# Hardware loops on ScalarE and VectorE, counts taken down by PE, 8-row casts and shared set-up buffers in a LoRA projection that moves 67 MB

## Chip, cores, metric

The kernel runs on one core of one Trainium2 chip. The metric is device time in microseconds (us), the median over executions. The profile's span (first to last instruction of the program) is about 1.3 us shorter than the time.

## The reference

```python
# x: 16 x 2048 x 256 f32 (32768 rows), W: 256 x 256, A: 256 x 16, B: 16 x 256, E: 16, scale = 1.0
y = x @ W + scale * (((x @ lora_A) * lora_E) @ lora_B)      # f32, 33.5 MB in and 33.5 MB out
```

The kernel folds the small factors into one matrix, weff = W + A·diag(E)·scale·B, once. Then it computes y = x·weff.

## The kernel before

The rows are cut into 4 chunks of 64 rows in each of 128 partitions. A chunk (8.39 MB) has a "home" in SBUF. x is loaded there, the result is written over it, and it is stored from there. There are three homes, so chunk 3 must wait for stores of chunk 0. All loads and stores are issued by SyncE in a fixed order.

```python
ORDER = [("A",), ("L", 0, 0, 8), ("L", 0, 8, 24), ("L", 0, 24, 40), ("L", 0, 40, 64),
         ("L", 1, 0, 32), ("L", 1, 32, 64), ("L", 2, 0, 16), ("L", 2, 16, 64),
         ("S", 0, 0, 40), ("S", 0, 40, 64), ("L", 3, 0, 32), ("L", 3, 32, 64),
         ("S", 1, 0, 64), ("S", 2, 0, 64), ("S", 3, 0, 64)]     # kind, chunk, rows from, to
HELD = (2, 16)                       # GpSimd stops at row 16 of chunk 2 ...
HOLDERS = (("S", 0, 0, 40),)         # ... until this store has landed
CG = 4                               # rows of one group; 64 groups in all
```

Each group goes through five steps: GpSimd casts it to bf16, PE turns it (4 matmuls), VectorE copies it out of PSUM, PE multiplies it (8 matmuls), and ScalarE copies the result into the home.

```python
# GpSimd, 64 times (waits for loads and for the hold: cut)
gpsimd.wait_ge(s_turned, g - NS + 1)
gpsimd.tensor_copy(out=stage[g % NS][:], in_=home(c)[:, b:b + CG, :]).then_inc(s_stage[g % UNROLL], 1)
# ScalarE, written out 64 times
scalar.wait_ge(s_y, g + 1)
scalar.copy(out=home(c)[:, b:b + CG, :], in_=psum_y[g % NY][:]).then_inc(s_free[(g + NY) % UNROLL], 1)
if g in ends:
    scalar.drain().then_inc(s_done, 1)          # releases a store
# PE, a hardware loop of 16 laps
with tensor.Fori(0, N_GROUPS // UNROLL):
    for i in range(UNROLL):
        turn(i + 1, i)
        multiply(i)
```

Of the kernel before, what the change touches and what calls it, by code (L numbers as in the profile page):

```python
# [7 lines left out]
P = 128  # L8
FP32 = mybir.dt.float32
BF16 = mybir.dt.bfloat16  # L10
# [3 lines left out]
ROWS = 64  # L14
N_CHUNKS = 4
N_HOMES = 3

ORDER = [
    ("A",),
    ("L", 0, 0, 8),  # L20
    ("L", 0, 8, 24),
    ("L", 0, 24, 40),
    ("L", 0, 40, 64),
    ("L", 1, 0, 32),
    ("L", 1, 32, 64),
    ("L", 2, 0, 16),
# [13 lines left out]
WARM_UP = 2  # L40

CG = 4
GPC = ROWS // CG
N_GROUPS = N_CHUNKS * GPC

NS, NX, NT, NY = 2, 2, 2, 2

UNROLL = 4
# [3 lines left out]
def kernel(  # L52
# [20 lines left out]
    y_chunks = out_flat.rearrange("(c p b) m -> c p b m", p=P, b=ROWS)  # L73

    sbuf, psum, sem = nc.alloc_sbuf_tensor, nc.alloc_psum_tensor, tc.alloc_semaphore
    homes = [sbuf(f"home{h}", [P, ROWS, K], FP32) for h in range(N_HOMES)]
    stage = [sbuf(f"stage{i}", [P, CG, K], BF16) for i in range(NS)]
    xt = [sbuf(f"xt{i}", [P, CG, P * KT], BF16) for i in range(NX)]
    ident = sbuf("ident", [P, P], FP32)

    w_sb = sbuf("w_sb", [P, KT, M], FP32)
    a_sb = sbuf("a_sb", [P, KT, R], FP32)
    b_sb = sbuf("b_sb", [R, M], FP32)
    e_sb = sbuf("e_sb", [R, 1], FP32)
    ate = sbuf("ate", [R, KT, P], FP32)
    weff = sbuf("weff", [P, KT, M], BF16)
    psum_xt = [psum(f"psum_xt{i}", [P, CG, P], FP32) for i in range(NT)]
    psum_y = [psum(f"psum_y{i}", [P, CG, M], FP32) for i in range(NY)]
# [8 lines left out]
    stored = {op: sem(f"stored_{op[1]}_{op[2]}") for op in ORDER if op in waited}  # L97
    stored_rest = nc.alloc_semaphore("stored_rest")
    n_rest = sum(op[0] == "S" and op not in waited for op in ORDER)
    ends = sorted((c * ROWS + e) // CG - 1 for kind, c, s, e in (op for op in ORDER if op[0] == "S"))  # L100
    s_ident = sem("ident_made")
    s_pe_set_up = sem("pe_set_up")
    s_ate = sem("ate_made")
    s_stage = [sem(f"staged{i}") for i in range(UNROLL)]
    s_turned = sem("turned")
    s_xt = [sem(f"xt_made{i}") for i in range(UNROLL)]
    s_y = sem("multiplied")
    s_free = [sem(f"y_free{i}") for i in range(UNROLL)]
    s_done = sem("rows_done")

    def home(c):
        return homes[c % N_HOMES]

    sync, gpsimd, scalar, vector, tensor = nc.sync, nc.gpsimd, nc.scalar, nc.vector, nc.tensor

# [19 lines left out]
    def sync_program():  # L135
        for n, op in enumerate(ORDER):
            if op[0] == "A":
                a = lora_A.rearrange("(q t) r -> q t r", t=KT)
                ins = sync.dma_start(out=a_sb[:], in_=a).then_inc(set_up_loaded["a"], 16)
                opening.append(ins.ins.name)  # L140
                continue
            kind, c, s, e = op
            at_home = home(c)[:, s:e, :]
            if kind == "L":
                for st in stored:
                    if st[1] == c - N_HOMES and st[2] < e and s < st[3]:
                        sync.wait_ge(stored[st], 16)
                ins = sync.dma_start(out=at_home, in_=x_chunks[c, :, s:e, :]).then_inc(loaded[op], 16)
                if n == 1:
                    opening.append(ins.ins.name)  # L150
            else:
                sync.wait_ge(s_done, ends.index((c * ROWS + e) // CG - 1) + 1)
                sync.dma_start(out=y_chunks[c, :, s:e, :], in_=at_home).then_inc(stored.get(op, stored_rest), 16)

    def gpsimd_program():
        gpsimd.memset(ident[:], 0.0).then_inc(s_ident, 1)  # L156
        gpsimd.wait_ge(s_ident, 1)
        gpsimd.affine_select(  # L158
            out=ident[:],
            in_=ident[:],  # L160
            compare_op=ALU.not_equal,
            fill=1.0,
            base=0,
            pattern=[[-1, P]],
            channel_multiplier=1,
        ).then_inc(s_ident, 1)
        for g in range(N_GROUPS):
            c, b = g // GPC, g % GPC * CG
            for op, landed in loaded.items():
                if op[1:3] == (c, b):  # L170
                    gpsimd.wait_ge(landed, 16)
            if (c, b) == HELD:
                for op in HOLDERS:
                    gpsimd.wait_ge(stored[op], 16)
            if g >= NS:
                gpsimd.wait_ge(s_turned, g - NS + 1)  # L176
            gpsimd.tensor_copy(out=stage[g % NS][:], in_=home(c)[:, b:b + CG, :]).then_inc(s_stage[g % UNROLL], 1)  # L177

        gpsimd.wait_ge(s_turned, N_GROUPS - NS + 1)
        gpsimd.drain().then_inc(s_stage[N_GROUPS % UNROLL], 1)  # L180

    def scalar_program():
        for name, to, of in (
            ("w", w_sb, W.rearrange("(q t) m -> q t m", t=KT)),
            ("b", b_sb, lora_B),
            ("e", e_sb, lora_E[:, None]),
        ):
            ins = scalar.dma_start(out=to[:], in_=of).then_inc(set_up_loaded[name], 16)
            opening.append(ins.ins.name)
        for g in range(N_GROUPS):  # L190
            c, b = g // GPC, g % GPC * CG
            scalar.wait_ge(s_y, g + 1)
            scalar.copy(out=home(c)[:, b:b + CG, :], in_=psum_y[g % NY][:]).then_inc(s_free[(g + NY) % UNROLL], 1)  # L193
            if g in ends:
                scalar.drain().then_inc(s_done, 1)  # L195

    def vector_program():
        vector.wait_ge(set_up_loaded["e"], 16)
        vector.wait_ge(s_pe_set_up, 1)
        vector.tensor_scalar(  # L200
            out=ate[:],
            in0=psum_y[0][:R, :KT, :P],
            scalar1=e_sb[:],
            scalar2=float(scale),
            op0=ALU.mult,
            op1=ALU.mult,
        ).then_inc(s_ate, 1)
        for g in range(N_GROUPS):
            vector.wait_ge(s_turned, g + 1)
            vector.tensor_copy(out=xt[g % NX][:], in_=psum_xt[g % NT][:].bitcast(BF16)).then_inc(s_xt[g % UNROLL], 1)  # L210
            if g == 0:
                vector.wait_ge(set_up_loaded["w"], 16)
                vector.wait_ge(s_pe_set_up, 2)
                vector.tensor_add(out=weff[:], in0=w_sb[:], in1=psum_y[1][:, :KT, :]).then_inc(s_free[0], 1)  # L214
                vector.drain().then_inc(s_free[1], 1)

    def tensor_program():
        def turn(i, result=None):
            words = stage[i % NS][:].bitcast(FP32)
            staged = s_stage[i % UNROLL]  # L220
            for b in range(CG):
                if b == 0:
                    tensor.wait_ge(staged, 1)
                if b == CG - 1 and result is not None:
                    tensor.wait_ge(s_free[result % UNROLL], 1)
                ins = tensor.transpose(psum_xt[i % NT][:, b, :], words[:, b, :], ident[:])  # L226
                if b == 0:
                    ins.then_inc(staged, -1)
            ins.then_inc(s_turned, 1)

        def multiply(i):
            turned, free = s_xt[i % UNROLL], s_free[i % UNROLL]
            for b in range(CG):
                for t in range(KT):
                    if b == t == 0:
                        tensor.wait_ge(turned, 1)
                    ins = tensor.matmul(  # L237
                        psum_y[i % NY][:, b, :],
                        xt[i % NX][:, b, t::KT],
                        weff[:, t, :],  # L240
                        start=(t == 0),
                        stop=(t == KT - 1),
                    )
                    if b == 0:
                        ins.then_inc((turned, free)[t], -1)
            ins.then_inc(s_y, 1)

        tensor.wait_ge(s_ident, 2)
        for i in range(WARM_UP):
            tensor.matmul(psum_y[1][:, :2, :], ident[:], ident[:, None, :].to_broadcast([P, 4, P]), start=True, stop=True)  # L250
        tensor.wait_ge(set_up_loaded["a"], 16)
        for t in range(KT):
            ins = tensor.transpose(psum_y[0][:R, t, :P], a_sb[:, t, :], ident[:])  # L253
        ins.then_inc(s_pe_set_up, 1)
        turn(0)
        tensor.wait_ge(set_up_loaded["b"], 16)
        tensor.wait_ge(s_ate, 1)
        for t in range(KT):
            ins = tensor.matmul(psum_y[1][:, t, :], ate[:, t, :], b_sb[:], start=True, stop=True)  # L259
        ins.then_inc(s_pe_set_up, 1)  # L260
        assert N_GROUPS % UNROLL == 0 and all(UNROLL % n == 0 for n in (NS, NX, NT, NY))
        with tensor.Fori(0, N_GROUPS // UNROLL):
            for i in range(UNROLL):
                turn(i + 1, i)
                multiply(i)

    def wait_for_stores(nc):
        nc.sync.wait_ge(stored_rest, 16 * n_rest).then_inc(stored_rest, -16 * n_rest)
# [44 lines left out]
```

## Time and profile before

| what | value | where |
|---|---|---|
| time, first 3 runs | 161.38 us (161.38 to 161.85) | timing |
| moved | 67.43 MB in all; the data queue takes 97.2% of 16 transfer engines' time | page, parts 2 and 3 |
| rate, 3 to 157 us | 433 GB/s | windows |
| PE busy | 59% of the span | page, part 1 |
| ScalarE per group | 1012 ns, then 0.30 us idle | groups, timeline |

From the page of the kernel before: the span, then, for 40 equal slices, the busy tenths of PE, ScalarE (ACT) and the mean of the 16 transfer engines, and the line of the data queue (packets, MB, share of 16 engines' span).

```profile
span 161.5 us, 2024 instructions
...
PE   2988999969999990000899999999910000000000
...
ACT  3003677747777772000157777777730000000000
...
DMA  7999999999999997998999999799799799699690
...
q1 hardware_dynamic: 2304, 67.13, 97.2%
```

The transfers are busy throughout. Compute stops twice: in the hold (about 62 to 76 us), and for good in the last quarter.

The timeline of SyncE's queue (start, length, what) shows when stores and the held loads were issued. A later window of the same view put the third of the last three stores at 118.69 us.

```profile
27.66 9.87 SPq L153 DMA_DIRECT2D out_dram<-home  x2
75.94 7.69 SPq L148 DMA_DIRECT2D home<-in_x_dram  x2
83.68 35.34 SPq L153 DMA_DIRECT2D out_dram<-home  x3
```

The last store is issued when about 19 us of earlier stores are still to be moved, by the prediction's estimate.

### The profile page before, as it was taken

The numbers are of one execution on the slowest core, as the hardware profiler recorded it, in microseconds if no ns is written. First come the engines' busy times: TensorE is split into PE (matmuls) and PEld (weight loads), VectorE is DVE, ScalarE is ACT, GpSimd is POOL, SyncE is SP. The second block draws the span as 40 slices with busy tenths as digits, with TensorE's granted clock in tenths as the row PEclk, the third lists the DMA queues.
The fourth block names the chain that finished last, engine by engine and source line by source line (L and its number), as shares of the span: only waits on it lengthen the run. The fifth ranks groups of instructions, "written<-read, shape, count | busy, mean of one in ns | idle before, by whom it ended". The sixth has DMA issues, their size and how long they took to land.

```text
span 161.5 us, 2024 instructions
## 1 busy us (share of the span) xinstructions
PE 95.4 (59%) x782; PEld 83.4 (52%) x782; DVE 45.4 (28%) x66; ACT 66.1 (41%) x65; POOL 66.9 (41%) x70
## 2 busy tenths in 40 slices
PE   2988999969999990000899999999910000000000
PEld 1347999959999990000789989999900000000000
DVE  0141555535555550000155555555400000000000
ACT  3003677747777772000157777777730000000000
POOL 1516768577778840001578777788200000000000
PEclk9975999999999999555599999999996555555555
DMA  7999999999999997998999999799799799699690
GB/s 253 405 438 452 402 452 446 446 406 446 394 548 414 402 390 337 477 467 371 420 459 440 406 446 536 319 519 471 308 503 487 308 503 503 292 503 503 292 519 16
DMA packets 2515, 67.43 MB, mean 418 GB/s; under 512 B 448, under 2 KB 464, under 8 KB 592
## 3 DMA queue, kind: packets, MB, share of 16 engines
q1 hardware_dynamic: 2304, 67.13, 97.2%
q10 hardware_dynamic: 208, 0.28, 0.6%
q14 instruction: 3, 0.02, 0.0%
HBM read 33.85 MB, written 33.55 MB: 417 GB/s over the span
## 4 chain that ended last, share of the span: by engine, by line
DMA 36%; PE 34%; POOL 1%; ACT 1%; issue 0%; SPq 0%; ACTq 0%; POOLq 0%
DMA out_dram<-home 30%; PE psum_y L237 22%; PE psum_xt L226 12%; DMA home<-in_x_dram 6%; POOL stage L177 1%; ACT home L193 1%; ACTq L195 0%; SPq L308 0%; POOLq L176 0%; SPq L272 0%
## 5 line engine op out<-in xcount | busy, mean ns | idle before, releaser
L193 ACT COPY home<-psum_y 128x1024 f32<-128x1024 f32 x64 | 64.8, 1012 | 50.5 <-PE psum_y L237 50.5
L177 POOL CAST stage<-home 128x1024 bf16<-128x1024 f32 x64 | 66.2, 1042 | 44.8 <-DMA out_dram<-home 17.5
L237 PE MATMUL psum_y<-weff,xt 128*128 128x256 bf16 x512 | 69.6, 281 | 0.0
L210 DVE COPY xt<-psum_xt 128x1024 bf16<-128x1024 bf16 x64 | 44.3, 692 | 63.4 <-PE psum_xt L226 63.4
L237 PEld LDWEIGHTS psum_y<-weff,xt 128*128 128x128 bf16 x512 | 51.8, 101 | 6.5
L226 PE MATMUL psum_xt<-ident,stage 128*128 128x128 f32 x260 | 41.4, 283 | 19.3 <-POOL stage L177 19.0
L226 PEld LDWEIGHTS psum_xt<-ident,stage 128*128 128x128 f32 x260 | 31.5, 146 | 22.1 <-issue 20.7
L250 PE MATMUL psum_y<-ident 128*128 128x512 f32 x4 | 3.7, 1078 | 2.9 <-POOL ident L158 2.9
L250 PEld LDWEIGHTS psum_y<-ident 128*128 128x128 f32 x4 | 1.2, 324 | 3.9 <-POOL ident L158 2.9
L200 DVE TENSOR_SCALAR ate<-psum_y,e_sb 16x256 f32<-16x256 f32 x1 | 0.5, 472 | 6.9 <-PE psum_y L253 6.9
L193 ACT ACT_TABLE_LOAD x1 | 1.3, 1283 | 2.1 <-SPq L272 2.1
L259 PE MATMUL psum_y<-b_sb,ate 16*128 16x256 f32 x4 | 1.1, 400 | 0.0
L156 POOL MEMSET ident<- 128x128 f32 x1 | 0.2, 205 | 1.7 <-SPq L272 1.7
L253 PEld LDWEIGHTS psum_y<-ident,a_sb 128*16 128x16 f32 x2 | 0.2, 114 | 1.2 <-issue 1.2
L214 DVE TENSOR_TENSOR weff<-w_sb,psum_y 128x512 bf16<-128x512 f32 x1 | 0.7, 687 | 0.4 <-PE psum_y L259 0.4
L259 PEld LDWEIGHTS psum_y<-b_sb,ate 16*128 16x128 f32 x4 | 0.7, 184 | 0.2 <-issue 0.2
L158 POOL TENSOR_SCALAR_AFFINE_SELECT ident<-ident 128x128 f32<-128x128 f32 x1 | 0.3, 293 | 0.2 <-POOL ident L156 0.2
L253 PE MATMUL psum_y<-ident,a_sb 128*16 128x128 f32 x2 | 0.4, 273 | 0.0
L294 POOL MEMSET const-float32-0.0<- 128x1 f32 x1 | 0.1, 99 | 0.2 <-issue 0.2
L294 POOL MEMSET const-bfloat16-1.0<- 128x1 bf16 x1 | 0.1, 103 | 0.0
L294 POOL MEMSET const-uint8-127<- 128x1 uint8 x1 | 0.1, 103 | 0.0
L294 POOL MEMSET const-float32-1.0<- 128x1 f32 x1 | 0.1, 99 | 0.0
## 6 DMA issues: line engine op xcount, KB each, us to landing
home<-in_x_dram SPq DMA_DIRECT2D x4, 4096.0 KB, 25.1
home<-in_x_dram SPq DMA_DIRECT2D x3, 2048.0 KB, 13.8
home<-in_x_dram SPq DMA_DIRECT2D x1, 6144.0 KB, 58.9
out_dram<-home SPq DMA_DIRECT2D x1, 5120.0 KB, 48.3
home<-in_x_dram SPq DMA_DIRECT2D x1, 3072.0 KB, 20.7
out_dram<-home SPq DMA_DIRECT2D x1, 3072.0 KB, 46.0
home<-in_x_dram SPq DMA_DIRECT2D x1, 1024.0 KB, 5.4
w_sb<-in_W_dram ACTq DMA_DIRECT2D x1, 256.0 KB, 3.0
```

Of the source, the lines that this page charges most:

```text
L158: gpsimd.affine_select(out=ident[:], in_=ident[:], compare_op=ALU.not_equal, fill=1.0, base=0, pattern=[[-1, P]], channel_multiplier=1,).t ...
L177: gpsimd.tensor_copy(out=stage[g % NS][:], in_=home(c)[:, b:b + CG, :]).then_inc(s_stage[g % UNROLL], 1)
L193: scalar.copy(out=home(c)[:, b:b + CG, :], in_=psum_y[g % NY][:]).then_inc(s_free[(g + NY) % UNROLL], 1)
L200: vector.tensor_scalar(out=ate[:], in0=psum_y[0][:R, :KT, :P], scalar1=e_sb[:], scalar2=float(scale), op0=ALU.mult, op1=ALU.mult,).then_in ...
L210: vector.tensor_copy(out=xt[g % NX][:], in_=psum_xt[g % NT][:].bitcast(BF16)).then_inc(s_xt[g % UNROLL], 1)
L214: vector.tensor_add(out=weff[:], in0=w_sb[:], in1=psum_y[1][:, :KT, :]).then_inc(s_free[0], 1)
L226: ins = tensor.transpose(psum_xt[i % NT][:, b, :], words[:, b, :], ident[:])
L237: ins = tensor.matmul(psum_y[i % NY][:, b, :], xt[i % NX][:, b, t::KT], weff[:, t, :], start=(t == 0), stop=(t == KT - 1),)
L250: tensor.matmul(psum_y[1][:, :2, :], ident[:], ident[:, None, :].to_broadcast([P, 4, P]), start=True, stop=True)
L253: ins = tensor.transpose(psum_y[0][:R, t, :P], a_sb[:, t, :], ident[:])
L259: ins = tensor.matmul(psum_y[1][:, t, :], ate[:, t, :], b_sb[:], start=True, stop=True)
L294: nc = _bacc.Bacc("TRN2", target_bir_lowering=False, num_devices=1)
```

## The change

The intent is a shorter program. ScalarE and VectorE run hardware loops whose waits are constants, because PE takes each count down again. PE also counts finished rows, which removes ScalarE's drains. GpSimd casts 8 rows at a time, and set-up tensors use a stage buffer that is still free. The core of the diff (set-up and renaming cut):

```diff
-    homes = [sbuf(f"home{h}", [P, ROWS, K], FP32) for h in range(N_HOMES)]
-    stage = [sbuf(f"stage{i}", [P, CG, K], BF16) for i in range(NS)]
+    ring = sbuf("ring", [P, RING, K], FP32)
+    stage = [sbuf(f"stage{i}", [P, CAST, K], BF16) for i in range(NS)]          # CAST = 8
+    spare = stage[1][:].bitcast(FP32)...                                        # w_sb, b_sb, ate live here
...
-                sync.wait_ge(s_done, ends.index((c * ROWS + e) // CG - 1) + 1)
+                sync.wait_ge(s_done, (c * ROWS + e) // CG + NY)
...
-            scalar.wait_ge(s_y, g + 1)
-            scalar.copy(out=home(c)[:, b:b + CG, :], in_=psum_y[g % NY][:]).then_inc(...)
-            if g in ends:
-                scalar.drain().then_inc(s_done, 1)
+        for n in (RING, N_CHUNKS * ROWS - RING):
+            with scalar.Fori(0, n // (UNROLL * CG)) as lap:
+                for i in range(UNROLL):
+                    scalar.wait_ge(s_y[i], 1)
+                    to = ring[:, bass.ds(lap * (UNROLL * CG) + i * CG, CG), :]
+                    scalar.copy(out=to, in_=psum_y[i % NY][:]).then_inc(s_free[(i + NY) % UNROLL], 1)
...
+        with vector.Fori(0, N_GROUPS // UNROLL):
...
+            updates = {                                  # of multiply(i), by matmul
+                (0, 1): (s_xt[i % UNROLL], -1), (1, 0): (s_free[i % UNROLL], -1),
+                (1, 1): (s_turned[i % UNROLL], -1), (2, 0): (s_y[(i - NY) % UNROLL], -1),
+                (2, 1): (s_done, 1), (3, 1): (s_y[i % UNROLL], 1)}
```

More of the change, by code (lines that the diff above doesn't have):

```diff
@@ L42 @@
 CG = 4
-GPC = ROWS // CG
-N_GROUPS = N_CHUNKS * GPC
+CAST = 2 * CG
+RING = N_HOMES * ROWS
+N_GROUPS = N_CHUNKS * ROWS // CG
 NS, NX, NT, NY = 2, 2, 2, 2
@@ L75 @@
     sbuf, psum, sem = nc.alloc_sbuf_tensor, nc.alloc_psum_tensor, tc.alloc_semaphore
-    homes = [sbuf(f"home{h}", [P, ROWS, K], FP32) for h in range(N_HOMES)]
-    stage = [sbuf(f"stage{i}", [P, CG, K], BF16) for i in range(NS)]
+    ring = sbuf("ring", [P, RING, K], FP32)
+    stage = [sbuf(f"stage{i}", [P, CAST, K], BF16) for i in range(NS)]
     xt = [sbuf(f"xt{i}", [P, CG, P * KT], BF16) for i in range(NX)]
     ident = sbuf("ident", [P, P], FP32)
-    w_sb = sbuf("w_sb", [P, KT, M], FP32)
     a_sb = sbuf("a_sb", [P, KT, R], FP32)
-    b_sb = sbuf("b_sb", [R, M], FP32)
     e_sb = sbuf("e_sb", [R, 1], FP32)
-    ate = sbuf("ate", [R, KT, P], FP32)
+    spare = stage[1][:].bitcast(FP32).rearrange("q (n s) k -> q n (s k)", s=2)
+    w_sb, b_sb, ate = spare[:, :KT, :], spare[:R, 2, :], spare[:R, 3, :].rearrange("r (t q) -> r t q", t=KT)
     weff = sbuf("weff", [P, KT, M], BF16)
@@ L99 @@
     n_rest = sum(op[0] == "S" and op not in waited for op in ORDER)
-    ends = sorted((c * ROWS + e) // CG - 1 for kind, c, s, e in (op for op in ORDER if op[0] == "S"))
     s_ident = sem("ident_made")
@@ L103, with rows @@
     s_ate = sem("ate_made")
-    s_stage = [sem(f"staged{i}") for i in range(UNROLL)]
-    s_turned = sem("turned")
+    s_weff = sem("weff_made")
+    s_stage = [sem(f"staged{i}") for i in range(NS)]
+    s_room = sem("stage_read")
+    s_turned = [sem(f"turned{i}") for i in range(UNROLL)]
     s_xt = [sem(f"xt_made{i}") for i in range(UNROLL)]
-    s_y = sem("multiplied")
+    s_y = [sem(f"multiplied{i}") for i in range(UNROLL)]
     s_free = [sem(f"y_free{i}") for i in range(UNROLL)]
     s_done = sem("rows_done")
-    def home(c):
-        return homes[c % N_HOMES]
+    def rows(c, s, e):
+        at = c % N_HOMES * ROWS
+        return ring[:, at + s:at + e, :]
     sync, gpsimd, scalar, vector, tensor = nc.sync, nc.gpsimd, nc.scalar, nc.vector, nc.tensor
@@ L142, in sync_program @@
             kind, c, s, e = op
-            at_home = home(c)[:, s:e, :]
+            at_home = rows(c, s, e)
             if kind == "L":
@@ L166, in gpsimd_program @@
         ).then_inc(s_ident, 1)
-        for g in range(N_GROUPS):
-            c, b = g // GPC, g % GPC * CG
+        n_casts = N_CHUNKS * ROWS // CAST
+        for n in range(n_casts):
+            c, b = n * CAST // ROWS, n * CAST % ROWS
             for op, landed in loaded.items():
@@ L174, in gpsimd_program @@
                     gpsimd.wait_ge(stored[op], 16)
-            if g >= NS:
-                gpsimd.wait_ge(s_turned, g - NS + 1)
-            gpsimd.tensor_copy(out=stage[g % NS][:], in_=home(c)[:, b:b + CG, :]).then_inc(s_stage[g % UNROLL], 1)
-        gpsimd.wait_ge(s_turned, N_GROUPS - NS + 1)
-        gpsimd.drain().then_inc(s_stage[N_GROUPS % UNROLL], 1)
+            if n == 1:
+                gpsimd.wait_ge(s_weff, 1)
+            if n >= NS:
+                gpsimd.wait_ge(s_room, n - NS + 1)
+            gpsimd.tensor_copy(out=stage[n % NS][:], in_=rows(c, b, b + CAST)).then_inc(s_stage[n % NS], 1)
+        gpsimd.wait_ge(s_room, n_casts - NS + 1)
+        gpsimd.drain().then_inc(s_stage[n_casts % NS], 1)
     def scalar_program():
@@ L185, in scalar_program @@
             ("b", b_sb, lora_B),
-            ("e", e_sb, lora_E[:, None]),
+            ("e", e_sb[:], lora_E[:, None]),
         ):
-            ins = scalar.dma_start(out=to[:], in_=of).then_inc(set_up_loaded[name], 16)
+            ins = scalar.dma_start(out=to, in_=of).then_inc(set_up_loaded[name], 16)
             opening.append(ins.ins.name)
-        for g in range(N_GROUPS):
-            c, b = g // GPC, g % GPC * CG
-            scalar.wait_ge(s_y, g + 1)
-            scalar.copy(out=home(c)[:, b:b + CG, :], in_=psum_y[g % NY][:]).then_inc(s_free[(g + NY) % UNROLL], 1)
-            if g in ends:
-                scalar.drain().then_inc(s_done, 1)
+        for n in (RING, N_CHUNKS * ROWS - RING):
[4 more added lines that the diff above has]
+                    scalar.copy(out=to, in_=psum_y[i % NY][:]).then_inc(s_free[(i + NY) % UNROLL], 1)
     def vector_program():
@@ L200, in vector_program @@
         vector.tensor_scalar(
-            out=ate[:],
+            out=ate,
             in0=psum_y[0][:R, :KT, :P],
@@ L207, in vector_program @@
         ).then_inc(s_ate, 1)
-        for g in range(N_GROUPS):
-            vector.wait_ge(s_turned, g + 1)
-            vector.tensor_copy(out=xt[g % NX][:], in_=psum_xt[g % NT][:].bitcast(BF16)).then_inc(s_xt[g % UNROLL], 1)
-            if g == 0:
-                vector.wait_ge(set_up_loaded["w"], 16)
-                vector.wait_ge(s_pe_set_up, 2)
-                vector.tensor_add(out=weff[:], in0=w_sb[:], in1=psum_y[1][:, :KT, :]).then_inc(s_free[0], 1)
-                vector.drain().then_inc(s_free[1], 1)
+        vector.wait_ge(s_turned[0], 1)
@@ new lines, in vector_program @@
+        vector.tensor_copy(out=xt[0][:], in_=psum_xt[0][:].bitcast(BF16)).then_inc(s_xt[0], 1)
+        vector.wait_ge(set_up_loaded["w"], 16)
+        vector.wait_ge(s_pe_set_up, 2)
+        vector.tensor_add(out=weff[:], in0=w_sb, in1=psum_y[1][:, :KT, :]).then_inc(s_free[0], 1)
+        vector.drain().then_inc(s_weff, 1)
+        with vector.Fori(0, N_GROUPS // UNROLL):
+            for i in range(UNROLL):
+                g = i + 1
+                vector.wait_ge(s_turned[g % UNROLL], 1)
+                vector.tensor_copy(out=xt[g % NX][:], in_=psum_xt[g % NT][:].bitcast(BF16)).then_inc(s_xt[g % UNROLL], 1)
@@ L217, in tensor_program @@
     def tensor_program():
         def turn(i, result=None):
-            words = stage[i % NS][:].bitcast(FP32)
-            staged = s_stage[i % UNROLL]
+            n, at = divmod(i, CAST // CG)
+            words = stage[n % NS][:].bitcast(FP32)
             for b in range(CG):
-                if b == 0:
-                    tensor.wait_ge(staged, 1)
+                if b == 0 and at == 0:
+                    tensor.wait_ge(s_stage[n % NS], 1)
                 if b == CG - 1 and result is not None:
@@ L225, in turn @@
                     tensor.wait_ge(s_free[result % UNROLL], 1)
-                ins = tensor.transpose(psum_xt[i % NT][:, b, :], words[:, b, :], ident[:])
-                if b == 0:
-                    ins.then_inc(staged, -1)
-            ins.then_inc(s_turned, 1)
+                ins = tensor.transpose(psum_xt[i % NT][:, b, :], words[:, at * CG + b, :], ident[:])
+                if b == 0 and at == 0:
+                    ins.then_inc(s_stage[n % NS], -1)
+            ins.then_inc(s_turned[i % UNROLL], 1)
@@ L231, in multiply @@
         def multiply(i):
-            turned, free = s_xt[i % UNROLL], s_free[i % UNROLL]
+            updates = {
+                (0, 1): (s_xt[i % UNROLL], -1),
+                (1, 0): (s_free[i % UNROLL], -1),
+                (1, 1): (s_turned[i % UNROLL], -1),
+                (2, 0): (s_y[(i - NY) % UNROLL], -1),
+                (2, 1): (s_done, 1),
+                (3, 1): (s_y[i % UNROLL], 1),
+            }
+            if (i + 2) % (CAST // CG) == 0:
+                updates[0, 0] = s_room, 1
@@ L235, in multiply @@
                     if b == t == 0:
-                        tensor.wait_ge(turned, 1)
+                        tensor.wait_ge(s_xt[i % UNROLL], 1)
                     ins = tensor.matmul(
@@ L243, in multiply @@
                     )
-                    if b == 0:
-                        ins.then_inc((turned, free)[t], -1)
-            ins.then_inc(s_y, 1)
+                    if (b, t) in updates:
+                        ins.then_inc(*updates[b, t])
         tensor.wait_ge(s_ident, 2)
         for i in range(WARM_UP):
-            tensor.matmul(psum_y[1][:, :2, :], ident[:], ident[:, None, :].to_broadcast([P, 4, P]), start=True, stop=True)
+            ins = tensor.matmul(
+                psum_y[1][:, :2, :], ident[:], ident[:, None, :].to_broadcast([P, 4, P]), start=True, stop=True
+            )
+            ins.then_inc(s_y[UNROLL - NY + i], 1)
         tensor.wait_ge(set_up_loaded["a"], 16)
@@ L253, in tensor_program @@
             ins = tensor.transpose(psum_y[0][:R, t, :P], a_sb[:, t, :], ident[:])
+            if t == 0:
+                ins.then_inc(s_free[1], 1)
         ins.then_inc(s_pe_set_up, 1)
@@ L258, in tensor_program @@
         for t in range(KT):
-            ins = tensor.matmul(psum_y[1][:, t, :], ate[:, t, :], b_sb[:], start=True, stop=True)
+            ins = tensor.matmul(psum_y[1][:, t, :], ate[:, t, :], b_sb, start=True, stop=True)
         ins.then_inc(s_pe_set_up, 1)
@@ L265, in tensor_program @@
                 multiply(i)
+        for i in range(NY):
+            tensor.wait_ge(s_free[i], 1).then_inc(s_done, 1)
     def wait_for_stores(nc):
```

## The prediction

> **What bounds it now.** DMA. The page gives 67.43 MB in a 161.5 us span; the data queue takes 97.2% of 16 engines' time. The windows view shows 433 GB/s from 3 to 157 us, the same with compute busy (427 to 441 GB/s, 83 to 117 us) as with every compute engine idle (419 to 446 GB/s, 125 to 155 us). [...] At 434 GB/s, 67.43 MB take 155.4 us. The other 6 us are the start (first data after 1.0 us, full rate by 2 us) and the end (data stop near 157.4 us, the store wait ends near 160, then the exit). No compute engine bounds it: PE is busy 59%, and none works after 118.7 us.
>
> **Slack of the compute chain.** Stores move behind what was issued before them. The first store (5 MB, about 12 us of data) is issued at 27.66 us and lands 48.3 us later: the loads of three chunks (25.2 MB, estimate: until about 60 us) are ahead of it, so it has about 30 us of slack. Chunk 2's store is issued at 97.7 us; at 19.3 us per 8.39 MB its data start at about 119 us: 21 us of slack. The last is issued at 118.7 us, its data start at about 138 us: 19 us. The chain of waits calls PE 34% critical because it follows the first store's issue; that is the end of a queue, not a bound.
>
> **What the change does to the chain.**
> - Casts of 8 rows: two of today's 1042 ns, so 2.08 us. The first work after an empty pipe (5.9, 11.5, 76.0 us) waits about 1.0 us more. In steady state two groups take PE 2 x 1.31 us, so the cast stays hidden.
> - Stage buffer 1 holds the set-up tensors: the second cast waits for weff (about 10.5 us), but its load lands only at 11.4 us. No cost.
> - Loops on ScalarE and VectorE: one back branch per four groups. [...] Even if dynamic addresses made ScalarE the slowest at 1.5 us a group, 32 groups would lose about 6 us, less than the slack.
> - PE counts finished rows two groups late: each store is issued 1.5 to 2.5 us later for that. With the cast, the first goes out at 29 to 31 us, chunk 2's at 99.5 to 102, the last at 119.5 to 122.
>
> All of this lies in slack of 19 us or more. Removed: instructions and drains, none on the path. Added to the critical path: nothing; bytes and load order stay, and the opening loads are still issued ahead of the entry barrier.
>
> **Predicted time**: 161.4 us, range 160.8 to 162.0. Chances: faster by over 2% 0.01, within 2% 0.97, slower by over 2% 0.02.
>
> **What would show it right.** About 433 GB/s from 3 to 157 us; 64 ScalarE copies still about 1012 ns; 32 casts of about 2.08 us; stores issued later as above, data stopping within 0.5 us of 157.4; the held loads still issued near 76 and 83 us.
>
> **What would show it wrong.** A hole in the DMA rate near 60, 119 or 138 us (a store issued too late[...]); a lower rate from the moved buffers; a start or exit changed by over 1 us with the number of instructions or semaphores; the first load no longer issued at 0.43 us.

The sum was 155.4 us of transfers, 6 us of start and end, and nothing for the change: 161.4 us. That the branches cost nothing is the author's estimate, and "1.5 us a group" is an allowance taken from no trace. The 434 GB/s is 8.39 MB in 19.3 us, as the packet records of the kernel before show it: in order of start, the 64 KB packets of the last three stores begin at 100.29, 119.69 and 139.01 us. With the mean of 433 GB/s the transfers would be 155.7 us (estimate, 67.43 MB over 433 GB/s). The same records show a store that moves behind what was issued before it: the first one, issued at 27.66 us, has its first packet at 61.54 us, when the last packet of the loads issued before it has begun (60.82 us).

## More of the kernel before

The groups of ScalarE and GpSimd (output <- input, count | busy us, mean ns | idle before) are:

```profile
L193 ACT COPY home<-psum_y 128x1024 f32<-128x1024 f32 x64 | 64.8, 1012 | 50.5 <-PE psum_y L237 50.5
L177 POOL CAST stage<-home 128x1024 bf16<-128x1024 f32 x64 | 66.2, 1042 | 44.8 <-DMA out_dram<-home 17.5
...
L193 ACT ACT_TABLE_LOAD x1 | 1.3, 1283 | 2.1 <-SPq L272 2.1
```

## The result and the profile after

The changed kernel took 162.06 us (161.82 to 162.42, 6 runs), beside 161.60 us for the kernel before. The ratio is 1.0026, with an interval of 1.0005 to 1.0046. A ratio here is the mean time of one kernel's fast runs over that of the other's of the same rounds, so it is not quite the ratio of the medians. The class "within 2%" was right. The time lies 0.06 us above the range.

The page of the changed kernel:

```profile
span 160.5 us, 2052 instructions
...
PE   2799978978979879400899798999990000000000
...
ACT  0008789788788897800167888777772000000000
...
DMA  7999999999999997989999999996996996996990
...
q1 hardware_dynamic: 2304, 67.13, 97.7%
...
L183 POOL CAST stage<-ring 128x2048 bf16<-128x2048 f32 x32 | 60.4, 1893 | 52.0 <-PE psum_y L255 26.1
L201 ACT COPY ring<-psum_y 128x1024 f32 x64 | 63.7, 1013 | 25.4 <-PE psum_y L255 25.2
...
L201 ACT ACT_TABLE_LOAD x12 | 15.4, 1283 | 17.2 <-PE psum_y L255 17.2
```

Two things stand out. ScalarE loads its function table 12 times (1283 ns each), once in every lap of its first loop, where before it loaded it once. And the profiled span is shorter than that of before although the median time is longer. The first profile of before was an execution of 162.84 us, slower than any of the timed ones above, so comparing the two spans is misleading.

ScalarE's timeline (start, length, what, idle before) shows what a lap looks like. From one table load to the next, 19.08 to 25.38, four groups take 6.30 us. That is 1.58 us a group in place of 1.31.

```profile
19.08 1.28 ACT L201 ACT_TABLE_LOAD   x1 [0.29 <-PE psum_y L255]
20.37 1.93 ACT L201 COPY ring<-psum_y 128x1024 f32 x2
22.77 1.01 ACT L201 COPY ring<-psum_y 128x1024 f32 x1 [0.47 <-PE psum_y L255]
24.08 1.01 ACT L201 COPY ring<-psum_y 128x1024 f32 x1 [0.30 <-PE psum_y L255]
25.38 1.28 ACT L201 ACT_TABLE_LOAD   x1 [0.29 <-PE psum_y L255]
```

SyncE's queue after, and then the last line of the same view for a window around 121 us:

```profile
30.07 9.27 SPq L156 DMA_DIRECT2D out_dram<-ring  x2
74.51 8.17 SPq L151 DMA_DIRECT2D ring<-in_x_dram  x2
82.72 39.43 SPq L156 DMA_DIRECT2D out_dram<-ring  x3
```

```profile
121.81 0.33 SPq L156 DMA_DIRECT2D out_dram<-ring  x1
```

The first store goes out at 30.07 us and the last at 121.81, inside the predicted stretches. No store came too late, and the mean rate from 3 to 157 us is 433 GB/s in both. So where does the time come from? The windows view does not answer this, because it shows the mean of 16 transfer engines. The kernel ends with the last one.

The trace has start, length and size of each packet but no engine number. In the traces of the first result, before and after, 363 of the 368 packets that can follow another begin within 15 ns of the end of one. So we took the packets of one engine to follow each other without a gap, and sorted those of the last three stores (64 KB each, 24 an engine) into 16 chains by their starts and ends. Sums of packet time above the median packet of 2.42 us show which chain was slowed. The following is our own sorting of two traces, not a view: first packet's start, last packet's end, excess. `null_before` is the kernel before, profiled again (161.65 us); `after_again` is the changed one (161.96 us). The sorting can swap two chains where their starts are close, as around 100.7 us here: with the slow packet of 155 ns put at the head of the chain that ends last, the excess of that chain is 1152 and 1459 ns.

```text
null_before, last four to end       after_again, last four to end
100.71  158.86   155 ns             100.65  158.64     4 ns
100.79  158.93   178 ns             100.66  158.75   155 ns
101.52  159.47     0 ns             100.67  158.77   124 ns
100.89  159.82   997 ns             100.82  160.08  1304 ns
```

Fifteen engines are done by 159.5 us or earlier. One engine is slower. In both traces its packets take about 2.57 us in place of 2.42 us, but only until about the time when the compute engines stop: seven or eight slow packets in a row up to the one that starts at 118.6 us before, and one more, to 121.2 us, after. This engine ends the kernel. Here is the excess of its first eleven packets in ns, in order of time (with the packet of 155 ns at the head; also our own sorting):

```text
null_before, from 100.7 us   155 146 155 150 164 136  80 160   3   0   3
after_again, from 100.7 us   155 164 155 169 146 174 136 169 173  14   3
```

While x is loaded there is hardly a trace of this: in `after_again`, 129 load packets of 32 KB begin between 30 and 40 us, with the pipeline full; their median is 1.213 us and none took more than 1.221 us. So the same PE work has an effect beside stores that it hardly has beside loads.

That gave theory A: compute work slows one transfer engine while it stores, and the changed kernel does more of it beside stores. The rivals were no real difference, a longer start or exit, and a direct cost of loops, counts or table loads.

### The profile page after: what moved, and what is told of

Same layout as the page of the kernel before. It is cut to its first block, busy times and chain, and to the rows that moved or that the text cites. A ratio compares the mean times of both kernels' runs of the same rounds, so it can differ in the third digit from the quotient of the medians.

```text
span 160.5 us, 2052 instructions
## 1 busy us (share of the span) xinstructions
PE 97.2 (61%) x782; PEld 83.0 (52%) x782; DVE 46.1 (29%) x67; ACT 79.1 (49%) x76; POOL 61.1 (38%) x38
## 4 chain that ended last, share of the span: by engine, by line
DMA 33%; PE 30%; ACT 8%; POOL 2%; issue 1%; ACTq 0%; SPq 0%; POOLq 0%
DMA out_dram<-ring 28%; PE psum_y L255 20%; PE psum_xt L235 10%; DMA ring<-in_x_dram 5%; ACT L201 4%; ACT ring L201 4%; POOL stage L183 2%; ACTq L201 0%; SPq L332 0%; POOLq L182 0%; SPq L296 0%
## 5 line engine op out<-in xcount | busy, mean ns | idle before, releaser
L183 POOL CAST stage<-ring 128x2048 bf16<-128x2048 f32 x32 | 60.4, 1893 | 52.0 <-PE psum_y L255 26.1
L201 ACT COPY ring<-psum_y 128x1024 f32 x64 | 63.7, 1013 | 25.4 <-PE psum_y L255 25.2
L224 DVE COPY xt<-psum_xt 128x1024 bf16<-128x1024 bf16 x64 | 44.2, 691 | 65.7 <-PE psum_xt L235 65.7
L235 PE MATMUL psum_xt<-ident,stage 128*128 128x128 f32 x260 | 43.6, 284 | 20.4 <-POOL stage L183 11.1
L201 ACT ACT_TABLE_LOAD x12 | 15.4, 1283 | 17.2 <-PE psum_y L255 17.2
L206 DVE TENSOR_SCALAR stage<-psum_y,e_sb 16x256 f32<-16x256 f32 x1 | 0.5, 472 | 7.2 <-PE psum_y L273 7.2
L281 PE MATMUL psum_y<-stage 16*128 16x256 f32 x4 | 1.1, 400 | 0.0
L215 DVE COPY xt<-psum_xt 128x1024 bf16<-128x1024 bf16 x1 | 0.7, 690 | 1.0 <-PE psum_xt L235 1.0
L218 DVE TENSOR_TENSOR weff<-stage,psum_y 128x512 bf16<-128x512 f32 x1 | 0.7, 689 | 0.4 <-PE psum_y L281 0.4
L281 PEld LDWEIGHTS psum_y<-stage 16*128 16x128 f32 x4 | 0.7, 184 | 0.2 <-issue 0.2
```

The lines of the kernel that those rows point to most:

```text
L183: gpsimd.tensor_copy(out=stage[n % NS][:], in_=rows(c, b, b + CAST)).then_inc(s_stage[n % NS], 1)
L201: scalar.copy(out=to, in_=psum_y[i % NY][:]).then_inc(s_free[(i + NY) % UNROLL], 1)
L206: vector.tensor_scalar(out=ate, in0=psum_y[0][:R, :KT, :P], scalar1=e_sb[:], scalar2=float(scale), op0=ALU.mult, op1=ALU.mult,).then_inc(s ...
L215: vector.tensor_copy(out=xt[0][:], in_=psum_xt[0][:].bitcast(BF16)).then_inc(s_xt[0], 1)
L218: vector.tensor_add(out=weff[:], in0=w_sb, in1=psum_y[1][:, :KT, :]).then_inc(s_free[0], 1)
L224: vector.tensor_copy(out=xt[g % NX][:], in_=psum_xt[g % NT][:].bitcast(BF16)).then_inc(s_xt[g % UNROLL], 1)
```

## The experiments

### Null, and the changed kernel again

`null_before` is the kernel before, timed against itself. `after_again` is the changed kernel. There is no edit in either.

> The kernel before, unchanged, timed against itself: shows what interval 5 rounds give where there is nothing to find. Every theory expects a ratio of 1.000 +- 0.002. Its profile also shows whether the first profile of before (span 161.5 us, one of 16 transfer engines ending at 161.06 us while the other fifteen end by 159.85) was an unlucky execution: theory A expects that here the engine that ends last is the one whose packets are about 150 ns longer while compute overlaps the stores after 99 us, ending near 159.8 us.

> The changed kernel, unchanged, again, 5 rounds on the same chip as the null. Theory A (time is the end of the slowest of 16 transfer engines; one engine's store packets take about 2.57 us in place of 2.42 us while the compute engines still work; in the changed kernel they work until about 121.7 us in place of 118.6 us): ratio 1.001 to 1.003, and in its profile 9 to 10 slow packets on one engine after 99 us (8 in before). Theory B (no real difference, runs scatter): 1.000 +- 0.001, like the null. Theory C (start or exit longer): the ratio is over 1.001 but the last packet of the slowest engine ends no later than in the null's profile.

The null gave 161.51 us, 0.9989 (0.9967 to 1.0012). The changed kernel gave 162.04 us, 1.0026 (1.0006 to 1.0047). So the small difference is repeated, and the null shows none. In its profile the slowest engine also ends 0.26 us later (160.08 against 159.82), so a cause in the exit alone is ruled out.

The profile shows how much PE work runs beside stores. The windows view gives busy time and, in brackets, the number of instructions of PE's matmuls (first pair of columns after the length). Between 62 and 82 us the queue holds stores of chunk 0; from about 99 us it holds the last three stores. First `null_before`, then `after_again`:

```profile
62.00:75.00 13.00, 0.00 (x0) 0.00 (x0) 0.00 (x0) 0.00 (x0) 0.48 (x1) 0.58 0.96 413
75.00:82.00 7.00, 6.30 (x33) 5.27 (x34) 1.72 (x3) 1.92 (x2) 3.94 (x5) 0.56 0.96 413
99.00:126.00 27.00, 17.56 (x161) 16.08 (x159) 8.68 (x13) 14.44 (x15) 11.19 (x11) 0.87 1.03 443
```

```profile
62.00:75.00 13.00, 3.82 (x34) 3.05 (x31) 2.07 (x3) 5.04 (x5) 0.40 (x1) 0.75 0.96 415
75.00:82.00 7.00, 5.36 (x25) 4.41 (x26) 1.38 (x2) 1.01 (x1) 4.76 (x3) 0.50 0.98 420
99.00:126.00 27.00, 21.55 (x198) 19.79 (x195) 11.52 (x17) 17.63 (x18) 11.84 (x7) 0.95 1.03 443
```

Before, 194 matmuls (0 + 33 + 161) run beside stores. After, 257 do. The slower ScalarE pushes work out of the loads' time, both ahead of the hold and at the end. Both parts show in the packets: between 60 and 75 us, those of the first store have an excess of 0 in `null_before` and of 145 ns in sum in `after_again`.

### Compute kept busy to the end

After its last group, each engine goes on working on scratch tiles; stores and outputs are untouched. `busy_all` has all four parts, `busy_pe` only the last, `busy_others` only the first three.

```diff
+        for n in range(35):                       # ScalarE; VectorE: 52 copies, GpSimd: 34 casts
+            scalar.wait_ge(s_busy[0], n)
+            scalar.copy(out=xt[0][:], in_=psum_y[0][:]).then_inc(s_busy[0], 1)
...
+        with tensor.Fori(0, 40):                  # PE, after its own loop
+            for _ in range(8):
+                tensor.matmul(psum_xt[1][:, :2, :], weff[:, 0, :P], weff[:, 0, :], start=True, stop=True)
```

> The kernel before, with all four compute engines kept busy after their last group on scratch tiles until about 155 us (outputs unaffected). Theory A: slow packets of one engine go on until the end, about 14 more of +0.15 us, so +2.0 us (ratio about 1.013). Rival (the slow packets up to 118.6 us have to do with something else than compute work, such as the waiting store queue): no change, 1.000 +- 0.002.

> The kernel before with PE alone kept busy after its last group until about 150 us (320 matmuls of 128x256 bf16 into a free bank; outputs unaffected). Theory A2 (it is PE's work that slows one transfer engine's stores): slow packets go on to about 150 us, +1.5 to +2.0 us, 1.010 to 1.013. Rival (it takes ScalarE, VectorE or GpSimd, or all together): 1.000 +- 0.002, hardly any slow packet after 119 us.

> The same with ScalarE, VectorE and GpSimd kept busy until about 153 us and PE left alone. Theory A2: no slow packets after 119 us, 1.000 +- 0.002. Rival: +1 to +2 us.

| run | time (us) | ratio (interval) | slowest engine's end | slow packets after 119 us |
|---|---|---|---|---|
| `busy_all` | 163.75 | 1.0135 (1.0111 to 1.0158) | 161.57 | +98 to +174 ns each, to 157 us |
| `busy_pe` | 163.20 | 1.0104 (1.0081 to 1.0127) | 161.22 | +117 to +136 ns each, to 151 us |
| `busy_others` | 161.84 | 1.0024 (1.0000 to 1.0047) | 159.72 | +23 to +37 ns each, to 152 us |

No store waits for any of this work, and yet it costs up to 2.2 us. Theory A holds, and PE is the main part of it. `busy_others` is not settled: its interval just reaches 1.0000. Its profile shows no later end, but its slowed engine also began the last stores 0.5 us earlier than in `null_before` (100.19 against 100.71 us) and gathered more excess (1.57 against 1.15 us). So the other three engines are not shown to cost nothing. The windows of these two, from 118 to 150 us, first `busy_pe`, then `busy_others`, show that the added work is what was intended:

```profile
118.00:150.00 32.00, 32.00 (x295) 28.69 (x294) 0.00 (x0) 0.00 (x0) 0.00 (x0) 1.00 1.00 430
```

```profile
118.00:150.00 32.00, 0.00 (x0) 0.00 (x0) 30.50 (x45) 31.00 (x32) 30.15 (x30) 0.54 1.00 434
```

The mean rates, 430 and 434 GB/s, hardly tell the two apart. One engine out of 16 that is 5% slower changes the mean by 0.3%.

### One engine after another

As above, but ScalarE (8 copies), GpSimd (8 casts), VectorE (12 copies) and PE (72 matmuls) work in turn, each waiting for the one before it.

> The kernel before; after its last group ScalarE, then GpSimd, then VectorE, then PE work alone for about 8 us each on scratch tiles (from about 118 to 151 us; outputs unaffected). A packet of the last stores takes 2.42 us, and 2.57 us on one engine while compute works. If one compute engine is the cause, three slow packets in its turn and none in the others' turns; if it is the activity of any, slow packets in all four turns; if it takes all four at once, none.

Packets had at most +28 ns in ScalarE's turn (its first one), +14 in GpSimd's and +31 in VectorE's, +37 where PE took over, and then, in PE's turn (143.9 to 154.6 us), +61, +51, +127 and +127 ns. So it is mainly PE. One more packet, begun at 154.8 us, had +155 ns although PE's last matmul was over. The closing instructions of the program run there, and the same is seen at the end of compute in `null_before` (+160 ns at 118.6) and `busy_others` (+146 ns at 152.3). That packet comes with the end of any of these kernels, so it doesn't tell them apart.

### Number of PE instructions or amount of PE work

After its last group PE runs 48 wide matmuls, then 320 narrow ones. At the end of the queue, 15 tiny loads of 1 to 15 partitions were meant to tell which engine is the slow one.

```diff
+        with tensor.Fori(0, 6):
+            for _ in range(8):
+                tensor.matmul(psum_y[1][:, :2, :], weff[:, 0, :P], weff[:], start=True, stop=True)        # 512 columns
+        with tensor.Fori(0, 40):
+            for _ in range(8):
+                tensor.matmul(psum_y[1][:, 0, :32], weff[:, 0, :P], weff[:, 0, :32], start=True, stop=True)
```

> The kernel before; after its last group PE runs 48 matmuls of 128x512 (about 10 us, 5 a us), then 320 of 128x32 (many more a us); at the end of the queue 15 tiny loads of 1 to 15 partitions[...]. If the number of PE instructions slows it: small or no excess (under 80 ns a packet) in the first phase and 150 ns or more in the second. If the columns that PE streams do: about 150 ns in the first phase and less in the second.

Windows of `pe_kinds`, the wide ones, then the narrow ones:

```profile
119.00:129.00 10.00, 9.72 (x42) 4.57 (x47) 0.00 (x0) 0.00 (x0) 0.00 (x0) 1.00 0.99 426
129.00:144.00 15.00, 14.75 (x322) 11.19 (x320) 0.00 (x0) 0.00 (x0) 0.00 (x0) 0.63 1.04 450
```

In the wide phase, packets of the slow engine took 50, 80 and 66 ns more. In the narrow phase they took 287 to 343 ns more. The wide phase streams about 2.4 times as many columns (48 x 512 against 320 x 32), and still slows the engine far less. So the columns are not what counts; within PE's work it is the number of instructions. Each matmul has its weight load, so the wide phase has 96 in 10 us, 24 in a packet of 2.48 us. The narrow phase has 640 in 15 us, 116 in a packet of 2.72 us. That is about 2.7 ns (65/24) and 2.6 ns (300/116) of delay for each PE instruction. In `busy_pe` it is also 2.6 ns (120 ns for about 46 in a packet).

So far this reads as an effect of PE alone, but the traces show more. Count, in all profiles but that of `relieve`, every recorded instruction of any engine, with its drains, semaphore and branch instructions, that begins during one of the 24 packets of the slowed engine. The excess follows this count (384 packets, correlation 0.95, 2.6 ns an instruction) better than that of PE's matmuls and weight loads alone (0.88). It fits what PE leaves unexplained: 14 packets of `busy_others` with 7 to 10 instructions and +27 ns on average, and the packet at 118.6 us in `null_before`, which has no matmul, 20 instructions of the program's end, and +160 ns. So PE may stand out only because it has the most instructions. This is a correlation: no run has another engine issue as many.

The slow engine took part in 11 of the 15 tiny loads. Which engine that makes it is not shown: our trace has no engine numbers. The time of this run, 165.93 us, contains the 15 loads themselves and is not compared.

### A slower ScalarE and nothing else

One more copy of a scratch tile in each group, in the kernel before; `slower_scalar` has a second, of 256 columns.

```diff
+            scalar.wait_ge(s_slow, g)
+            scalar.copy(out=slow[:], in_=weff[:]).then_inc(s_slow, 1)       # 128x512 bf16
```

> The kernel before with one more ScalarE copy (128x512 bf16, to a scratch tile) after each group's copy, so that a group takes about 1.6 us in place of 1.31 us: no loop, no count on PE, no table load in a lap, nothing of the changed kernel but a slower ScalarE. No store waits for it (the last is issued near 127 us, its data start near 138 us). Theory A2: the groups pushed into the stores' time (about 9 before the hold, 3 to 4 at the end) bring about 12 x 1.31 us more of PE work beside stores at about 6% each: +0.8 to +1.1 us, 1.005 to 1.007. Rival (work off the chain costs nothing while stores are issued in time): 1.000 +- 0.002.

> As slow_scalar, with a second extra ScalarE copy (128x256) in each group, so that a group takes about 1.75 us and PE ends near 127 us in place of 116 to 117. The last store is still issued 10 us before its data start. About 100 more matmuls than before run beside stores; at 6.5 ns of delay each (155 ns in a packet of 2.57 us with 9.2 matmuls a us): +0.6 us, 1.003 to 1.005. Rival (a slower ScalarE costs nothing while stores are issued in time): 1.000 +- 0.002.

`slow_scalar` gave 161.64 us, 1.0007 (0.9990 to 1.0024). That is a miss of our expectation. The added copy overlaps the copies on both sides by about 0.1 us, so a group took 1.43 us where we had expected 1.6, PE ended at 119.0 us, and 213 matmuls ran beside stores in place of 194; the dose was too small to decide anything. `slower_scalar` gave 162.31 us, 1.0045 (1.0005 to 1.0084), with the slowest engine's end at 160.49 us. Its windows:

```profile
62.00:75.00 13.00, 7.27 (x57) 5.65 (x57) 3.46 (x5) 11.23 (x20) 3.12 (x3) 0.97 0.97 420
75.00:82.00 7.00, 5.74 (x32) 4.80 (x33) 1.52 (x3) 2.41 (x4) 4.21 (x5) 0.57 1.03 441
99.00:126.00 27.00, 23.58 (x186) 18.58 (x184) 10.55 (x16) 26.89 (x47) 14.08 (x14) 1.00 1.03 444
```

There are 275 matmuls beside stores in place of 194. There are no loops and no counts on PE, and still it is as slow as the changed kernel, though the interval only just leaves out 1. A slower ScalarE alone, for which no store waits, is enough. The added copies are instructions beside stores too, so this run does not separate them from the PE work that they move.

### The table loads

In the changed kernel, one copy of a single column ahead of the loops:

```diff
+        scalar.wait_ge(s_weff, 1)
+        scalar.copy(out=table[:], in_=weff[:, 0, :1])
         for n in (RING, N_CHUNKS * ROWS - RING):
             with scalar.Fori(0, n // (UNROLL * CG)) as lap:
```

> The changed kernel with one ScalarE copy of one column ahead of its loops, so that the activation table is loaded once and not in each of 12 laps. All theories expect 1 table load in place of 12 (14 us of ScalarE time gone). Theory A: compute ends near 119 to 120 us in place of 121.7, one slow packet fewer, time lower than the changed kernel by 0.1 to 0.2 us. Rival: the table loads themselves disturb the transfers, time down to that of before or below. Theory C: no change of the time.

> The changed kernel a third time, beside table_once_2 on one chip: 1.002 to 1.004 of the kernel before, as twice before.

> The changed kernel with one table load, a second time. PE work beside stores back at the level of before (193 matmuls there, 243 in the changed kernel): theory A2 expects 0.2 to 0.35 us less than after_3, 1.000 to 1.002 of the kernel before. Rival (the loops, the counts on PE or the larger casts cost it): as after_3.

The groups of ScalarE in `table_once` confirm the edit:

```profile
L204 ACT COPY ring<-psum_y 128x1024 f32 x64 | 64.8, 1012 | 42.9 <-PE psum_y L258 42.9
L198 ACT ACT_TABLE_LOAD x1 | 1.3, 1283 | 2.1 <-SPq L299 2.1
```

Its windows have 195 matmuls beside stores (0 + 28 + 167), as in the kernel before:

```profile
62.00:75.00 13.00, 0.00 (x0) 0.00 (x0) 0.00 (x0) 0.20 (x1) 0.56 (x1) 0.60 0.96 413
75.00:82.00 7.00, 5.52 (x28) 4.49 (x29) 1.38 (x2) 1.12 (x2) 4.76 (x3) 0.53 0.97 417
99.00:126.00 27.00, 18.12 (x167) 16.59 (x164) 9.68 (x14) 15.10 (x15) 9.47 (x5) 0.94 1.02 442
```

| chip | changed kernel | with one table load | before |
|---|---|---|---|
| first | 162.04, 1.0026 (1.0006 to 1.0047) | 161.78, 1.0022 (0.9996 to 1.0049) | 161.49 |
| second | 162.17, 1.0047 (1.0007 to 1.0086) | 161.95, 1.0011 (0.9974 to 1.0049) | 161.57 |

The mean over the 12 executions of each is 0.34 us lower with one table load (standard error 0.14). In the profiles the slowest engine ends at 159.73 and 159.84 us with one load, near before's 159.82. In the changed kernel the slowed engine ends at 159.98, 160.08 and 160.12. The table loads are most of the difference that the profiles show. They act by the work that they move, hardly by themselves: in the profile after, only those at 63.20 and 82.11 us begin near stores. Whether the rest of the change costs something too is not settled: with one table load the kernel is still 0.26 us above before on average (28 executions of before, standard error 0.13), and both its intervals contain 1.

### Moving the hold

`no_hold` sets `HELD = None`. `hold_longer` sets `HOLDERS = (("S", 0, 0, 40), ("S", 0, 40, 64))`.

> The kernel before without its hold of GpSimd at row 16 of chunk 2: compute fills 60 to 76 us, which was idle, and is limited at the end by the last load (lands at 101 us), so it ends near 113 us in place of 117.6. Theory A in its simple form (only compute beside the last three stores costs): two slow packets fewer, 0.3 us faster, 0.998. If compute beside the first stores (60 to 76 us) slows an engine as well, the gain is cancelled: 1.000 +- 0.002, with slow packets between 62 and 76 us in the trace.

> The kernel before with the hold lengthened until the second store of chunk 0 has landed too (82 us in place of 74 to 76): compute ends near 124 us in place of 117.6. Theory A: two to three more slow packets on one engine among the last stores, +0.3 to +0.5 us, 1.002 to 1.003, as in the changed kernel without any of its edits. Rival (start, exit or something else of the changed kernel costs the 0.4 us): 1.000 +- 0.001.

`no_hold` gave 162.31 us, 1.0037 (1.0011 to 1.0064). It fills the idle stretch, but beside stores: 327 matmuls run there, and slow packets appear from 63 us on. Its compute ended at 119.9 us and not near 113 as we had expected; why was not followed up. `hold_longer` gave 162.03 us, 1.0014 (0.9986 to 1.0043), which doesn't decide. In its profile 233 matmuls run beside stores and the slowest engine ends at 160.27 us.

### Relieving the slow engine

The last 4 rows of the last store were issued as two transfers, of partitions 120 to 127 and of 0 to 119. The author assumed that this relieves one engine and gives others more; no trace here shows how partitions are shared out among engines. The first outcome below ("it ends about 1.2 us earlier") is for a slow engine that is the relieved one.

> The kernel before with the last 4 rows of the last store issued apart: partitions 120 to 127 in one transfer of 8 partitions, partitions 0 to 119 in another of 120[...]. [...] it ends about 1.2 us earlier, the last engine ends near 159.0 to 159.4 us in place of 159.8, 0.4 to 0.8 us faster, 0.995 to 0.9975. If it is another engine: no change or 0.1 us more.

It took 161.72 us, 1.0011 (0.9992 to 1.0030). Fifteen engines ended their last packet of that store by 157.94 us and the slow one at 158.39. The slow one then still had nine 4 KB packets to move (128 of them over 16 engines would be eight each), and ended at 159.80. So the slow engine was not relieved; it had more than an even share. No experiment beat the kernel before.

## Why the prediction was wrong

- **The step that failed is "All of this lies in slack of 19 us or more … Added to the critical path: nothing."** Slack in the order of stores was real: nobody waited. But compute was not free here while stores ran. Beside stores, each PE instruction went with a delay of about 2.6 ns on one transfer engine, and in most profiles the kernel ended with that engine. The term set to 0 should have been, as our estimate, about 63 matmuls and as many weight loads more beside stores, 126 x 2.6 ns = 0.33 us; with the instructions of all engines, 154 more, it is 0.40 us. The profiles show 0.16 to 0.30 us at the slowed engine. The medians differ by 0.46, 0.55 and 0.60 us, so the term accounts for a good part of the difference, and not surely for all of it. None of the signs that the prediction had listed as showing it wrong was seen; it had no sign for this term.
- **What moved that work was overlooked**: twelve table loads of 1283 ns. The prediction costed the loop as one back branch for four groups and took it as hidden, and no run here isolates one. The trace after shows table loads of 1283 ns each, one in each of the 12 laps of the first loop and none in the second. The allowance for a slow ScalarE of "1.5 us a group" was near the measured 1.58, but only its effect on when stores are issued was asked.
- **The centre was too low and the range too narrow.** It rested on three executions (161.38). Later medians of the same kernel lie between 161.49 and 161.81, and single timed ones between 161.19 and 162.78. About a third of the miss from 161.4 to 162.06 is this: 0.2 us to the 161.60 of the same rounds.
- **Right**: the transfers bind. The first store was issued at 30.07 us (predicted 29 to 31), the last at 121.81 (119.5 to 122). Chunk 2's, at 102.03, was just past its stretch (99.5 to 102). The held loads went out at 74.5 and 82.3. The casts took 1893 ns, a little less than the 2.08 us expected, and stayed hidden: PE waited for a cast three times, 11.1 us in all, 9.9 us of it at the end of the hold. Sharing the stage buffer cost no wait beyond a load's landing: in the trace after, weff is done at 10.48 us, and the second cast begins at 10.89 us, when its load has landed. The class was right.
- **A reading that misled**: "data stop near 157.4 us" came from the windows view. The last packet ended at 159.8 us in typical executions of before. That view gives the mean of 16 engines; the slowest one was invisible in it.

**Open.** How instructions reach a transfer engine, and whether PE's differ from others in this, is not shown. Nor is it shown whether the profiler's recording of each instruction takes part. Each of the six executions of the first result lists a span and a clock, so recording may have been on in the timed ones too; no run was made with it surely off. If it is the recording, the effect belongs to the measurement and not to the kernel. Also open: the 0.26 us that remain on average with one table load, and whether the slow engine is always the same one. In one of three profiles of the changed kernel another engine, which began 1.7 us late, ended even later (160.45 against 160.12).

## What to carry to other kernels

When transfers bind, ask which of the 16 engines ends last and what else runs while it works; a mean rate hid 1 us on one engine here. "Off the critical path" answers who waits for whom, not what concurrent work costs, so at the level of a few tenths of a per cent cost the work that moves into the time of stores as well. That holds for executions measured as these were; whether it holds without the recording is open. When a straight run of ScalarE instructions becomes a hardware loop, check in the trace whether the table load is in the lap (12 loads in 12 laps here, 1283 ns each); one small activation ahead of the loop brought them to 1 in `table_once`.
